# Up projections of the middle block as seven block products, with new weight sums and a spilled convolution

## The chip, the cores and the metric

One of the cores of a Trainium2 chip runs the program. The metric is the device time of one execution in microseconds; the time of a kernel is the median of several runs. TensorE (PE) multiplies, VectorE (DVE) and ScalarE (ACT) do the element-wise work, GpSimd (POOL) does little here, and SyncE (SP) issues every DMA, in the order of the program, on one queue.

## The reference

One layer of a hybrid decoder works on 2128 positions (16 meta tokens, 2048 prompt tokens, 64 sample tokens) of 1024 channels, in float32. A token-mixing block (input projection to 5 x 1024 columns, a causal convolution of width 31 with a layer norm, a pooling branch, gates, an output projection) is followed by a gated feed-forward part. The feed-forward part is what the change touches most:

```python
h2 = rmsnorm(x, norm2_g)
up = h2 @ w_up                                  # 1024 -> 2 x 2816
up, new_ffn = causal_dwconv(up, prev_ffn, ffn_dw)   # width 3
v, g = up[..., :D_FF], up[..., D_FF:]
x = x + (jax.nn.gelu(g) * v) @ w_down           # 2816 -> 1024
```

## The kernel before

**Tiling.** Channels lie on the 128 partitions (8 chunks, index c), positions on the free axis. The positions are cut into three blocks b of 708, 708 and 712; a matmul takes one half of a block (354 or 356 columns, 356 or 358 with the two columns of history that the width-3 convolution needs). The sample tokens are the last 64 columns of block 2.

**Precision.** Each operand is split into a high part of type fp32r (copied by ACT) and the remainder (subtracted by DVE). A product of two such operands is three matmuls: low x high, high x low, high x high. All of PE's work on weights has line L212.

**Units and tasks.** The program is a list of units, each one weight tile with its matmuls and the work on its results. For block b the order is: pooling and gate projections (PG), convolution projections (C), output projection (WO), for b = 1 then the gate and value projections of block 2 (G), and the feed-forward part (FF). FF works on value/gate couples f = 0 to 21, in groups; the down projection (DN) of a group is placed behind the first couple of the next group, and the last one at the end (`up_end` marks its start). Norms, convolutions (`conv_norm`, `conv_pair`), weight sums and the like are tasks, generators that `drip` steps in order of their creation while DVE's planned time (class `Pace`) is behind PE's. `force` finishes a task that a unit needs. A task can yield until `room(k)` holds: at most 52 tiles of one size, "s" in the profile, share one pool, and three are kept in reserve.

**Weights.** A weight tile ("wb") holds both parts, 2 x 1024 columns, 1 MB. There are four such buffers (`W_BUFS`, L51), taken in turn. A weight is loaded as "raw" and split when it is used for the first time, and the split tile is stored to HBM ("keep"). Later uses load it from there. `w_loads` (L275) issues the loads in the order of use, at most LEAD = 4 units ahead of the unit last named to `w_start` (L311), and one unit fewer for weights that are known in HBM. A load into a buffer has to wait for the last matmul that reads the tile that was there.

**Pairs.** In block 2 (`MIXED`), the couples f = 3 to 21 are computed by `pair` (L964): the 8 input chunks are seen as 2 halves and the two halves of the columns as 2 halves, so that value and gate of one couple are a 2 x 2 block product, computed with 7 block products of 12 matmuls instead of 8. The operands are sums: `mixed_rows` makes those of the activations, the task `mixed_weights` those of the weights, seven parts of 512 columns for each f, split, and stored in HBM in the order of use (m1 to m3 of two parts, m4 of one). A pair uses its four PSUM banks x, a, bb, d in this order:

```python
prod(x, 0, 0, b11, True)
prod(a, 0, h, mx[1], True)
prod(bb, 1, 0, mx[3], True)
prod(d, 1, h, mx[2], True)
prod(x, 2, 0, b21, False)
prod(bb, 2, h, mx[4], False)
prod(a, 3, 0, b22, False)
```

The second argument is the number of the weight tile (0 for m1 to 3 for m4). After product 4, DVE forms a sum that is shared, and the value and the gate come out of five such sums, of 358 columns each. Block 2 works in groups of 6, 6, 5, 5 couples (`MIX_GROUPS`), blocks 0 and 1 in groups of 6, 5, 5, 6, where a couple is two plain units of 48 matmuls.

**Order around the change.** `mixed_weights` starts with PG of block 1, is the last in the list of tasks, and is barred from WO of block 1 to shortly after the start of G. The convolutions of block 2 can start in G and end in FF of block 1. In `MIXED` blocks the residual x1 is kept in HBM between groups (`spill`, `fetch`).

## Time and profile before

| what | us |
|---|---|
| median of 3 runs | 3002.84 |
| lowest, highest run | 2999.94, 3004.23 |
| the profiled execution, its own time | 3004.2 |
| its span, first to last instruction | 3002.1 |
| busy PE | 2938.3 |
| busy DVE | 2042.8 |
| busy ACT | 821.2 |

The span is the stretch that the profile covers; the own time of that execution is 2.1 us longer. A row of the profile names the line, the engine, the operation and the tiles ("out<-in"), then the count, the busy time and the mean duration of one in ns, and at the end how long the engine was idle before and what released it. Matmuls are pipelined: the mean duration of one is longer than the distance from one to the next. Lines L180, L184 and L195 are helpers through which nearly all of DVE's and ACT's work goes, so that tiles tell more than lines.

Where the stages of blocks 1 and 2 begin (first L212 matmul, us from the start of the span): PG of block 1 at 1155, C at 1309, WO at 1434, G at 1499, FF at 1627; PG of block 2 at 2150, C at 2294, WO at 2418, FF at 2483.

### The profile page before, as it was taken

What the parts mean: (1) busy time and instruction counts of PE and PEld (TensorE: products, weight loads), DVE (VectorE), ACT (ScalarE), POOL (GpSimd) and SP (SyncE); (2) the same over time, 40 slices, a digit from 0 to 9 for tenths busy, and PEclk for the clock granted to TensorE, in tenths of its full rate; (3) what the DMA queues carried; (4) which work ended last, traced back from release to release, by engine and by line L of the source; (5) the groups of instructions that cost most, each with busy time, mean ns of one, the idle gap of its engine ahead of it and who ended that gap; (6) DMA issues with size and microseconds to landing.
All of it is one profiled execution on the core that took longest, in us unless ns stands there. A gap on an engine that the chain in (4) does not pass through costs nothing.

```text
span 3002.1 us, 44205 instructions
## 1 busy us (share of the span) xinstructions
PE 2938.3 (98%) x17928; PEld 2924.6 (97%) x17928; DVE 2042.8 (68%) x3006; ACT 821.2 (27%) x1238; POOL 108.8 (4%) x201
## 2 busy tenths in 40 slices
PE   7999999999999998999999999999999999999998
PEld 7999999999999998999999999999999999999997
DVE  7998998679996456653489999655652137544645
ACT  4201334233223232432221212223241113221312
POOL 0111100020000000000010000000000000000000
PEclk9999999999999999999999999999999999999999
DMA  7424554955655557888743444799743376777686
GB/s 283 160 71 161 196 207 162 335 212 173 229 189 197 204 191 286 274 321 277 277 154 120 163 136 146 266 320 328 266 170 138 139 267 215 255 268 263 236 302 242
DMA packets 187755, 660.41 MB, mean 220 GB/s; under 512 B 30880, under 2 KB 39200, under 8 KB 145696
## 3 DMA queue, kind: packets, MB, share of 16 engines
q1 hardware_dynamic: 187552, 657.59, 62.2%
q8 instruction: 141, 2.31, 0.3%
q14 instruction: 62, 0.51, 0.0%
HBM read 433.35 MB, written 224.17 MB: 219 GB/s over the span
## 4 chain that ended last, share of the span: by engine, by line
PE 81%; DVE 12%; ACT 2%; DMA 2%; issue 2%; SPq 0%; DVEq 0%; ACTq 0%
PE ps L212 81%; DVE s L184 8%; DVE s L180 2%; DVE wb L180 2%; ACT s L195 2%; DMA wb<-keep 1%; DMA s<-in_x 0%; ACT wb L195 0%; DMA out_ffn_s<-sf 0%; DMA raw<-in_w_in 0%; SPq L204 0%; DVE s L189 0%; DMA raw<-in_w_dn 0%; SPq L208 0%; DVE rs L184 0%
## 5 line engine op out<-in xcount | busy, mean ns | idle before, releaser
L212 PE MATMUL ps<-s,wb 128*128 128x356 f32 (+2 forms) x17628 | 2904.4, 326 | 32.3 <-DMA wb<-keep 11.7
L212 PEld LDWEIGHTS ps<-s,wb 128*128 128x128 f32 x17628 | 2886.3, 189 | 43.2 <-DVE s L180 19.4
L184 DVE SCALAR_TENSOR_TENSOR s<-s,half,s 128x708 f32<-128x708 f32 (+1 forms) x720 | 622.5, 928 | 0.0
L195 ACT ACTIVATE s<-s 128x708 fp32r<-128x708 f32 (+8 forms) x447 | 316.2, 715 | 829.9 <-DVE s L184 465.8
L180 DVE TENSOR_TENSOR s<-s,s 128x708 f32<-128x708 f32 (+10 forms) x526 | 402.4, 779 | 102.5 <-ACT s L195 92.7
L180 DVE TENSOR_TENSOR s<-s,ps 128x708 f32<-128x708 f32 (+4 forms) x225 | 159.7, 719 | 289.9 <-PE ps L212 233.5
L195 ACT ACTIVATE s<-ps 128x358 f32<-128x358 f32 (+4 forms) x197 | 117.5, 603 | 696.4 <-PE ps L212 679.8
L184 DVE SCALAR_TENSOR_TENSOR s<-ps,cst,s 128x708 f32<-128x708 f32 (+1 forms) x188 | 179.0, 953 | 91.6 <-ACT s L195 88.0
L184 DVE SCALAR_TENSOR_TENSOR s<-s,cst,s 128x712 f32<-128x712 f32 (+3 forms) x188 | 156.5, 845 | 88.2 <-ACT s L195 81.0
L180 DVE TENSOR_TENSOR wb<-raw,wb 128x1024 fp32r<-128x1024 f32 (+3 forms) x136 | 152.9, 1126 | 41.0 <-ACT wb L195 40.6
L195 ACT ACTIVATE wb<-raw 128x1024 fp32r<-128x1024 f32 (+3 forms) x136 | 132.2, 977 | 157.4 <-PE ps L212 92.3
L195 ACT ACTIVATE s<-ps,cst 128x708 f32<-128x708 f32 (+1 forms) x94 | 79.4, 847 | 272.9 <-PE ps L212 266.5
L184 DVE SCALAR_TENSOR_TENSOR s<-s,ps 128x708 f32<-128x708 f32 (+5 forms) x65 | 43.8, 695 | 144.1 <-PE ps L212 124.8
L184 DVE SCALAR_TENSOR_TENSOR s<-s,s 128x708 f32<-128x708 f32 (+2 forms) x96 | 85.5, 891 | 73.4 <-ACT s L195 71.6
L180 DVE TENSOR_TENSOR s<-raw,s 128x512 fp32r<-128x512 f32 x114 | 74.5, 687 | 60.8 <-ACT s L195 52.5
L195 ACT ACTIVATE s<-raw 128x512 fp32r<-128x512 f32 x114 | 68.2, 626 | 86.9 <-DMA raw<-in_w_up 68.7
L180 DVE TENSOR_TENSOR s<-s 128x722 f32<-128x722 f32 (+6 forms) x64 | 55.3, 863 | 28.2 <-ACT s L195 20.5
L200 POOL COPY s<-phist 128x15 f32<-128x15 f32 x24 | 16.5, 687 | 1080.4 <-PE ps L212 1023.8
L184 DVE SCALAR_TENSOR_TENSOR sc<-sa,cst,sc 128x64 f32<-128x64 f32 x232 | 46.9, 280 | 0.3
L195 ACT ACTIVATE s<-s,half 128x708 f32<-128x708 f32 (+1 forms) x48 | 46.5, 975 | 0.8
L195 ACT ACTIVATE s<-s,cst 128x712 f32<-128x712 f32 x38 | 33.7, 886 | 40.4 <-DVE s L180 38.4
L200 POOL CAST s<-hhist 128x2 fp32r<-128x2 f32 x48 | 17.5, 396 | 607.8 <-PE ps L212 389.8
(51 smaller groups left out, 369.5 us busy)
## 6 DMA issues: line engine op xcount, KB each, us to landing
wb<-keep SPq DMA_DIRECT2D x227, 1024.0 KB, 5.0
keep<-wb SPq DMA_DIRECT2D x100, 1024.0 KB, 6.3
keep<-s SPq DMA_DIRECT2D x266, 256.0 KB, 5.7
raw<-in_w_up SPq DMA_DIRECT2D x82, 512.0 KB, 5.7
wb<-keep SPq DMA_DIRECT2D x40, 640.0 KB, 5.2
wb<-keep SPq DMA_DIRECT2D x32, 768.0 KB, 5.2
raw<-in_w_in SPq DMA_DIRECT2D x40, 512.0 KB, 5.2
s<-in_x SPq DMA_DIRECT2D x40, 354.0 KB, 7.6
```

The costliest lines, as they stand in the source:

```text
L180: nc.vector.tensor_tensor(out=out, in0=a, in1=b, op=op)
L184: nc.vector.scalar_tensor_tensor(out=out, in0=a, scalar=s, in1=b, op0=op0, op1=op1)
L195: nc.scalar.activation(out, a, func, **kw)
L200: nc.gpsimd.tensor_copy(out, a)
L212: nc.tensor.matmul(out, lhsT=lhsT, rhs=rhs, start=start, stop=stop, skip_group_check=again)
```

## The change

Block 1 gets the pairs too, with groups of its own (5, 5, 4, 4, 4); couples 0 to 2 stay plain in both blocks. The two halves of a value and gate weight that are used unsummed are no longer stored again: a pair takes them from the split weights that block 0 stored ("up" with f, and the second half of "up" with 22 + f, called "half"). `mixed_weights`, now one task for each f, makes only the four sums, in one HBM tile of 2048 columns, of which "s13" is the first half and "s24" the second. So the seven products are computed in the same order, with other weight tiles, and the loads of the next pair are issued at other places:

```diff
-        w = [W((f"m{i}", f), None, h if i == 4 else 2 * h) for i in range(1, 5)]
+        w = [W(("up", f), A["w_up"][f]), W(("s13", f), None, 2 * h), W(("s24", f), None, 2 * h), W(("half", FC + f), None, h)]
...
             prod(x, 0, 0, b11, True)
...
-            prod(a, 0, h, mx[1], True)
-            w_start(w[1])
+            prod(a, 1, 0, mx[1], True)
...
-            prod(bb, 1, 0, mx[3], True)
+            prod(bb, 1, h, mx[3], True)
...
-            prod(d, 1, h, mx[2], True)
-            w_start(w[2])
+            prod(d, 2, 0, mx[2], True)
...
-            prod(x, 2, 0, b21, False)
+            prod(x, 0, h, b21, False)
+            w_start(w[2], 0)
...
-            prod(bb, 2, h, mx[4], False)
-            w_start(w[3])
+            prod(bb, 3, 0, mx[4], False)
...
-            prod(a, 3, 0, b22, False)
-            w_start(w[3] + 1)
+            prod(a, 2, h, b22, False)
+            w_start(w[3] + 1, 0)
```

The second argument of `w_start` is new; with 0, known weights may be loaded four units ahead, as others are.

```diff
-            if q.known and wstate["load"] >= wstate["first"] + LEAD - 1:
+            if q.known and wstate["load"] >= wstate["first"] + LEAD - wstate["late"]:
```

The weight sums, without the three unsummed parts:

```diff
-            yield from part(a11, "m1", 0, 2 * h)
-            yield from part(a12, "m3", 0, 2 * h)
-            yield from part(a22, "m3", h, 2 * h)
...
-            yield from part(s3, "m2", 0, 2 * h)
+        yield from part(s3, h)
...
-            yield from part(a21, "m1", h, 2 * h)
-            yield from part(a11, "m2", h, 2 * h)
-            yield from part(a12, "m4", 0, h)
+        yield from part(a21, 0)
+        yield from part(a11, 2 * h)
+        yield from part(a12, 3 * h)
+        kept["sums", f] = dst
```

These tasks stand ahead of the convolutions in the list now. Each pair needs the sums of its own f instead of all of them. The activations of block 1 get a norm of their own (`norm2_mixed`, which also sends the residual to HBM), and `mixed_rows` forms their sums from the split halves (`summed`).

The convolutions of block 2 ("last block") no longer stay in "s" tiles. Their inputs go to HBM when G has made them, are loaded again two chunks at a time, and the results go to HBM until the layer norm, which waits for the start of block 1's last down projection:

```diff
+            if b == SPILLED:
+                yield at(a)
+                R["ad", c] = dpool.tile([P, HC + n], F32, tag=f"ad_{c}", name=f"ad_{c}")
+                store(R["ad", c], a)
...
-        yield from room(2)
+        yield from room(4 if b == SPILLED else 2)
+        if b == SPILLED:
+            for cc in (c, c + 1):
+                a = R["a", b, cc][0] = S(HC + n)
+                load(a, R["ad", cc])
...
+        while b == SPILLED and now["i"] < mark["up_end", b - 1]:
+            yield "cond", lambda: now["i"] >= mark["up_end", b - 1]
...
+                    load(R["cv", b, cc], R["cvd", cc])
```

More of the change, by code (lines that the diff above doesn't have):

```diff
@@ L249, in trunk @@
     wsplits = {}
-    wstate = {"load": 0, "split": 0, "done": 0, "raws": 0, "first": 0}
+    wstate = {"load": 0, "split": 0, "done": 0, "raws": 0, "first": 0, "late": 1}
     def known(key):
+        if key[0] in ("s13", "s24", "half"):
+            t = kept.get((("up" if key[0] == "half" else "sums"), key[1]))
+            return None if t is None else t[:, :, :D] if key[0] == "s13" else t[:, :, -D:] if key[0] == "s24" else t[:, :, D // 2 :]
         if key[0] != "dn":
@@ L613, in conv_norm @@
                 tt(acc, acc, cv, ALU.add)
+            del cv
+            if b == SPILLED and c:
+                yield at(acc)
+                for cc in (0, 1) if c == 1 else (c,):
+                    R["cvd", cc] = dpool.tile([P, W], F32, tag=f"cvd_{cc}", name=f"cvd_{cc}")
+                    store(R["cvd", cc], R.pop(("cv", b, cc)))
+        while b == SPILLED and now["i"] < mark["up_end", b - 1]:
+            yield "cond", lambda: now["i"] >= mark["up_end", b - 1]
         yield at(acc)
@@ L622, in src @@
         def src(c):
+            for cc in range(c, min(c + AHEAD, KC)):
+                if ("cv", b, cc) not in R:
+                    yield from room(1)
+                    R["cv", b, cc] = S(W)
+                    load(R["cv", b, cc], R["cvd", cc])
             if c == 0:
@@ L865, in mixed_rows, with row_sums @@
-        del R["xt", b]
-    def mixed_weights():
+            rows = R["xt", b] if ("xt", b) in R else [summed(b, c) if c % (KC // 2) == k else None for c in range(KC)]
+            yield from row_sums(b, rows[k], rows[k + KC // 2])
+            del rows
+        R.pop(("xt", b), None)
+    def row_sums(b, x0, x1):
+        n, ops = hw(b) + 2, R["mx", b]
+        b11, b12 = halves(x0, b)
+        b21, b22 = halves(x1, b)
+        ta, tb = S(2 * n), S(2 * n)
+        t1, t2, t3, t4 = ta[:, :n], ta[:, n:], tb[:, :n], tb[:, n:]
+        tt(t1, b12, b11, ALU.subtract)
+        tt(t2, b22, t1, ALU.subtract)
+        tt(t3, b22, b12, ALU.subtract)
+        tt(t4, b21, t2, ALU.subtract)
+        del x0, x1, b11, b12, b21, b22
+        yield at(ta)
+        for t, (i, j) in ((ta, (1, 2)), (tb, (3, 4))):
+            hi, lo = S(2 * n, F32R), S(2 * n, F32R)
+            act(hi, t, AF.Copy)
+            yield at(hi)
+            tt(lo, t, hi.bitcast(F32), ALU.subtract)
+            ops[i].append((hi[:, :n], lo[:, :n], hi, lo))
+            ops[j].append((hi[:, n:], lo[:, n:]))
+            yield
@@ new lines, in mixed_weights, with part @@
+        yield from room(MIX_ROOM)
+        v, g = (pace.alloc("raw", RAW_BUFS, wpool.tile([P, 2 * h], F32, tag="raw", name=nm("raw"), bufs=RAW_BUFS)) for _ in range(2))
+        load(v, A["w_up"][f])
+        load(g, A["w_up"][FC + f])
+        a11, a12, a21, a22 = v[:, :h], v[:, h:], g[:, :h], g[:, h:]
+        yield at(g)
+        dst = dpool.tile([P, 2, 4 * h], F32, tag=f"sums_{f}", name=f"sums_{f}")
+        def part(t, c):
+            calm = lambda: pace.free["dma"] < pace.free["pe"]
+            yield "room", calm
+            yield from room(MIX_ROOM)
+            hi, lo = S(h, F32R), S(h, F32R)
+            act(hi, t, AF.Copy)
+            yield at(hi)
+            tt(lo, t, hi.bitcast(F32), ALU.subtract)
+            yield at(lo)
+            store(dst[:, 0, c : c + h], hi.bitcast(F32))
+            store(dst[:, 1, c : c + h], lo.bitcast(F32))
@@ L1317, in FF @@
         mark["FF", b] = len(units)
-        ws = [w_up(0), w_up(FC), w_up(1)]
+        plain = PLAIN.get(b, FC)
+        ws = [w_up(0), w_up(FC), w_up(1)] if plain else []
         holds = [[] if len(parts) > 1 else None for _ in ws]
-        for ts_ in parts:
+        for ts_ in parts if plain else ():
             i = len(units)
@@ L1326, in FF @@
         f0, pend = 0, None
-        for gs in MIX_GROUPS if b in MIXED else F_GROUPS:
+        for gs in MIX_GROUPS.get(b, F_GROUPS):
             for f in range(f0, f0 + gs):
-                if b in MIXED and f >= PLAIN:
+                if f >= PLAIN.get(b, FC):
                     pair(b, f)
@@ L1369, in trunk @@
         for ts_ in parts.get(b, (BOTH,)):
-            add_task(("h2", b, ts_), norm2(b, ts_))
+            add_task(("h2", b, ts_), norm2_mixed(b) if b in MIXED and ts_ == BOTH else norm2(b, ts_))
         if b in MIXED:
-            add_task(("mx", b), mixed_rows(b), after=[("h2", b, parts[b][-1]), ("mw",)])
+            add_task(("mx", b), mixed_rows(b), after=[("h2", b, parts.get(b, (BOTH,))[-1])])
         for ts_ in SPLIT if b == NBLK - 1 else (BOTH,):
@@ L1378, in trunk @@
             if b + 1 == SBLK:
+                for f in range(min(PLAIN.values()), FC):
+                    add_task(("mw", f), mixed_weights(f), mark["PG", 1], [("mw", f - 1)] if f > min(PLAIN.values()) else ())
                 for c in range(KC):
@@ L1470, in trunk @@
         for i, q in reversed(list(enumerate(wq))):
[L1471 removed]
+            parts_ = [("dn", q.key[1], f) for f in range(*q.key[2:])] if q.key[0] == "dn" else [("up" if q.key[0] == "half" else q.key[0], *q.key[1:])]
             q.again = all(k in last for k in parts_)
```

120 lines of the change are left out of this document (62 added, 58 removed).

## The prediction

> **What bounds the kernel now.** I read the page first, then the stages, then single pairs of units in the timeline.
>
> ```profile
> PE 2938.3 (98%) x17928; PEld 2924.6 (97%) x17928; DVE 2042.8 (68%) x3006; ACT 821.2 (27%) x1238; POOL 108.8 (4%) x201
> ...
> PE 81%; DVE 12%; ACT 2%; DMA 2%; issue 2%; SPq 0%; DVEq 0%; ACTq 0%
> ...
> L212 PE MATMUL ps<-s,wb 128*128 128x356 f32 (+2 forms) x17628 | 2904.4, 326 | 32.3 <-DMA wb<-keep 11.7
> ```
>
> PE is busy in 98% of the span and waits little, so the time is the number of matmuls times their spacing, plus PE's waits. Columns of the next view (stages, by the order of the L212 matmuls): PE, PEld, DVE, ACT, POOL busy, clock, DMA share, GB/s. The rows are block 2's gate and value projections with block 1's second norm; block 1's feed-forward part; block 2's pooling part.
>
> ```profile
> 1512.00:1637.00 125.00, 125.00 (x774) 125.00 (x773) 120.14 (x355) 20.46 (x33) 9.37 (x33) 1.00 0.43 154
> 1637.00:2162.00 525.00, 522.95 (x3217) 522.25 (x3217) 408.67 (x530) 135.36 (x192) 0.20 (x1) 1.00 0.65 224
> 2162.00:2303.00 141.00, 140.59 (x866) 140.13 (x865) 65.60 (x96) 46.60 (x74) 7.25 (x15) 1.00 0.50 175
> ```
>
> Block 1's feed-forward part, where the change lands, is bound by PE; DVE has 116 us free in it and 75 us in the stage behind it. Now PE's own timeline, the first row from block 1, the others from block 2's pairs:
>
> ```profile
> 1639.78 222.44 PE L212 MATMUL ps<-s,wb 128*128 128x356 f32 x1360
> ...
> 2589.70 72.99 PE L212 MATMUL ps<-s,wb 128*128 128x358 f32 x446
> 2663.23 14.11 PE L212 MATMUL ps<-s,wb 128*128 128x358 f32 x84 [0.54 <-DVE s L180]
> 2677.87 14.11 PE L212 MATMUL ps<-s,wb 128*128 128x358 f32 x84 [0.54 <-DVE s L180]
> ```
>
> The spacing is 222.44/1360 = 0.1636 us in block 1 and 72.99/446 = 0.1637 in block 2, so a product of a pair (12 matmuls) takes 1.96 us. A pair of block 2 is 84 matmuls, 13.75 us, but pairs follow each other by 2677.87 - 2663.23 = 14.64: each loses 0.89 us at one place, its sixth product, behind DVE's sum of product four.
>
> **Part 1, what is removed.** Nineteen of block 1's 22 value/gate couples shrink from 96 matmuls to 84: 228 fewer, 228 x 0.1636 = **-37.3 us**, all on the path.
>
> **Part 2, the weight buffers.** This step decides. A pair has four weights in a ring of four buffers, loaded in order on SP's queue. Before, each is used by neighbouring products: m1 by 1 and 2, m2 by 3 and 4, m3 by 5 and 6, m4 by 7. SP's timeline in the same pairs:
>
> ```profile
> 2665.51 0.32 SPq L204 DMA_DIRECT2D wb<-keep  x1
> ...
> 2667.52 0.38 SPq L204 DMA_DIRECT2D wb<-keep  x1
> ...
> 2671.43 0.32 SPq L204 DMA_DIRECT2D wb<-keep  x1
> ...
> 2675.39 5.08 SPq L204 DMA_DIRECT2D wb<-keep  x2
> ```
>
> Product 6 starts at 2663.23; 6 ends at 2665.20, 7 at 2667.16, and the next pair's 2 and 4 at 2671.09 and 2675.02. The loads go out 0.31 to 0.37 us after just these ends: **a load is issued when the last product on its buffer is over** (0.33 us below). The next pair's m1 leaves five products, 9.8 us, before its use.
>
> After the change, weight 1 ("up") serves products 1 and 5, weight 2 ("s13") 2 and 3, weight 3 ("s24") 4 and 7, weight 4 ("half") 6. The next pair's "up" can only go out after product 5 and is wanted after 6 and 7, that is 3.93 us later. "s13" stands behind it on SP and is wanted 5.89 us after product 5. Two loads of that size, issued back to back into an idle queue (SP's timeline, then the DMA issues of two short windows; the last column is the time to landing):
>
> ```profile
> 2509.69 0.82 SPq L204 DMA_DIRECT2D wb<-keep  x2
> ```
>
> ```profile
> wb<-keep SPq DMA_DIRECT2D x1, 1024.0 KB, 4.7
> ```
>
> ```profile
> wb<-keep SPq DMA_DIRECT2D x1, 1024.0 KB, 6.9
> ```
>
> The second is issued 0.49 us after the first and lands 7.4 us after the first's issue. From landing to matmul, in the chain of waits:
>
> ```profile
> 2170.02 6.26 DMA wb<-keep
> 2176.28 0.14 issue
> 2176.41 3.66 PE ps L212 x21
> ```
>
> So with product 5's end as zero, product 1 can start at 0.33 + 4.7 + 0.13 = 5.16 instead of 3.93, and product 2 at 0.33 + 7.4 + 0.13 = 7.86 instead of 5.89. "s24" goes out at 3.93 + 0.33 and is wanted at 7.86 + 2 x 1.96 = 11.78, 7.5 us later: in time. **Each step from pair to pair waits 7.86 - 5.89 = 1.97 us.** In block 2 the old 0.89 us lies inside this wait (it falls on product 6, after zero), so the net there is 1.08.
>
> The groups (5, 5, 4, 4, 4) with plain couples 0 to 2, and a down projection behind the first pair of each later group, give 14 such steps in block 1: 14 x 1.97 = **+27.6**. Block 2 keeps (6, 6, 5, 5), but runs the same new pair: 15 steps, 15 x 1.08 = **+16.2**. The other pairs follow plain units or a down projection, whose weights come earlier; five of them are in block 1, where each may lose block 2's 0.89: 0 to 4.4, I take **+2**, since block 1 has no sample columns in that DVE chain. Nine times a pair is followed by a down projection whose first weight (512 to 768 KB) replaces "up". Alone it lands about 3.4 to 4.05 us after issue (an estimate: 4.7 less the missing KB at the 2.7 us that the second megabyte took above); with 0.46 around it, that is 0 to 0.6 past 3.93: **+2**, bounds 0 to 6.
>
> The Trainium skill, DMA: Bandwidth & Descriptors, section "Anatomy of one DMA", fits 2.0 us plus bytes over 436 GB/s: an estimate of 4.4 us for one such load and 2.4 for the next one's bytes. The trace's 4.7 and 2.7 are worse on both, so the sum goes by the trace; by that page the wait would be 1.4 and the whole sum about nothing.
>
> **Part 3, DVE.** Rows by shape:
>
> ```profile
> L184 DVE SCALAR_TENSOR_TENSOR s<-s,half,s 128x648 f32<-128x648 f32 x240 | 197.6, 887 | 0.0
> ...
> L180 DVE TENSOR_TENSOR s<-s,ps 128x708 f32<-128x708 f32 x88 | 76.8, 888 | 93.6 <-PE ps L212 93.5
> L180 DVE TENSOR_TENSOR s<-raw,s 128x512 fp32r<-128x512 f32 x114 | 74.5, 687 | 60.8 <-ACT s L195 52.5 <-PE ps L212 6.1 <-DMA keep<-s 1.3
> ...
> L180 DVE TENSOR_TENSOR s<-s,ps 128x358 f32<-128x358 f32 x57 | 29.8, 523 | 37.1 <-ACT s L195 21.7 <-PE ps L212 15.3
> ...
> L180 DVE TENSOR_TENSOR s<-s,s 128x358 f32<-128x358 f32 x50 | 25.7, 528 | 0.8
> ```
>
> Block 1 adds five half-width sums per pair (19 x 5 x 0.525 = 50 us), the row sums (4 x 8 x 0.525 + 8 x 0.9 = 24) and eight adds for a fifth group (7). The weight sums fall from 11 DVE operations of 0.69 for each f to 8, and start as tasks ahead of the convolutions. How far they got before the window in which they are barred (DVE and ACT operations on their raw tile; ten of DVE's for one f):
>
> ```profile
> 1150.00:1200.00 50.00, 7.82 (x12) 4.69 (x8) 0.90 0.83 304
> ...
> 1350.00:1400.00 50.00, 13.21 (x20) 6.18 (x11) 1.00 0.99 340
> 1400.00:1450.00 50.00, 2.06 (x3) 1.88 (x3) 1.00 0.74 266
> ```
>
> About two f per 50 us at a DMA share up to 0.99. With 12 instead of 18 transfers of 256 KB worth for one f the same pace makes 13 or 14 of 19 there, the rest in the next projections, ahead of the convolutions. Before, ten f (76 us of DVE) fell behind 1446; after, about five (28). The three stages above held 594 us of DVE work in 791; they get 50 + 24 + 7 - 48 = 33 more. This is hidden under PE: **0**, with 164 us of cover. The 0.8 us of one convolution tap ahead of a pair's sum also lies inside the new 1.97 us.
>
> **Part 4, DMA.** Block 1's pairs load 3.5 MB in some 15.7 us, about 230 GB/s; the stages of the page ran at up to 340. On SP's queue come: eight stores of "a" (347 KB) during block 2's projections; eight loads of them and eight stores of results (365 KB) in the pairs; eight loads back while the last down projection and the pooling part run; residual spills per group, beside down projections, as block 2 has them now. Sixteen transfers in the pairs at 2.7 us a megabyte are about 1 us each when they stand ahead of a wanted weight: 0 to 16, I take **+4** for one in four. Block 2's small state transfers (40 KB, two in and two out per pair) meet the new loads too: 0 to 15, **+3**.
>
> **Sum:** -37.3 + 27.6 + 16.2 + 2 + 2 + 3 + 4 = +17.5. The profiled execution (span 3002.1, its own time 3004.2) becomes 3021.7; it stood 1.4 above the median 3002.84, so I forecast **3020 us** (own range 3009 to 3035).
>
> **Rivals.** (a) *The second load comes sooner*, that is, "s13" lands a plain 4.7 us after its own issue at 0.82 and only "up" is waited for: 1.23 per step, 14 x 1.23 + 15 x 0.34 - 37.3 + 11 = -4, **2999**. For it: the queue is idle at that moment. Against: the 6.9 above, with the queue idle too. Chance 0.16. The Trainium skill's fit, cited in part 2, leads to about the same place. (b) *Loads in time, faster*: if "up" went out two products earlier, only block 2's DVE wait would remain in block 1: -37.3 + 19 x 0.89 + 2 = -18, **2984**. It decides at 3.93 us from release to use; against it, no megabyte in the rows above lands in under 4.7. Chance 0.14. (c) *The convolutions starve*: each channel pair needs four free buffers of 52, while h2, row sums and f hold some 40. A channel pair is 60 x 0.823 = 49 us of DVE (197.6/240). One unfinished pair fits into the 75 us free in the pooling part beside the layer norm; from the second on, block 2's convolution projection waits 49 us: **3069**. Chance 0.10. (d) *No matmul goes*, or the waits cancel elsewhere: **3003**, 0.04.
>
> **How the numbers follow.** Forecast 0.56. A measurement of this kernel can tell about 0.2%, 6 us, from no change. Faster: (b) and a fifth of (a), 0.17. Same: the rest of (a), (d), and the forecast's low end, 0.21. Slower: 0.62. The range 2990 to 3045 takes in (a), the bounds of parts 2 and 4 and half of (c); it leaves out (b).
>
> **What the changed profile would show.** L212's matmuls: 17,400. In both blocks' pairs, PE idle of about 1.2 us before product 1 and 0.7 before product 2, both released by DMA wb<-keep, and SP issuing two loads together 0.33 us after product 5; pair to pair 15.7 to 15.9 us. The 0.54 us behind DVE goes where a pair follows a pair. keep<-s falls from 266 stores to 152. I am wrong if "up" is issued well before product 5 ends, if PE idles behind DVE or at the convolution projection, or if block 2's pairs stay at 14.64.

## The result and the profile after

The changed kernel takes 3042.11 us (median of 4 runs, 3034.23 to 3042.36), the kernel before 3003.53 in the same session (4 runs). The ratio is 1.0123, with an interval of 1.0104 to 1.0142. The span of the profiled execution went from 3002.1 to 3040.6 us: **+38.5**, where the forecast had +17.5. Slower was right and the time lies in the range, but the loss is more than twice what was forecast, and it came by other waits; that the range holds it is luck.

The page of the changed kernel, the lines that were shown of before (line numbers have moved by one: L213 is the matmul, L181 and L185 are DVE's, L196 is ACT's):

```profile
PE 2925.5 (96%) x17700; PEld 2900.5 (95%) x17700; DVE 2082.2 (68%) x3116; ACT 831.5 (27%) x1281; POOL 100.0 (3%) x169
...
PE 29%; DVE 7%; DMA 5%; ACT 1%; issue 1%; SPq 0%; DVEq 0%; ACTq 0%
...
L213 PE MATMUL ps<-s,wb 128*128 128x354 f32 (+2 forms) x17400 | 2891.0, 328 | 83.3 <-DMA wb<-keep 25.2
```

The matmuls that were to go are gone: 17,628 - 17,400 = 228. But PE's idle time ahead of them grew from 32.3 us to 83.3. (The chain's shares add up to 43% here; the chain was followed back over less than half of the span, so I don't read it.) Where the time came from shows by stage. I counted the L213 matmuls in their order, which gives each stage's start and length:

| stage | before, us | after, us | difference | forecast |
|---|---|---|---|---|
| FF of block 1 | 523.2 | 549.5 | +26.3 | about -2 |
| PG of block 2 | 143.8 | 151.3 | +7.5 | 0 |
| FF of block 2 | 505.8 | 512.7 | +6.9 | about +20 |
| all else | | | -2.2 | 0 |

So the two feed-forward parts missed in opposite directions. The windows of FF of block 1 and of PG of block 2 (columns as in the prediction):

```profile
1624.00:2174.00 550.00, 504.33 (x2949) 495.46 (x2949) 453.77 (x618) 138.74 (x222) 1.47 (x2) 0.97 0.80 278
...
2174.00:2325.00 151.00, 148.04 (x912) 147.24 (x912) 83.70 (x135) 49.13 (x77) 9.97 (x16) 0.99 0.46 165
```

PE was busy for 522.95 of 525 us there before and is idle for 46 of 550 now; the DMA share went from 0.65 to 0.80, and the granted clock from 1.00 to 0.97. PE's waits in that stage (us in total, times, longest):

```profile
PE ps L213 <- DMA wb<-keep: 13.8, 5, 4.3
PE ps L213 <- DVE s L181: 11.1, 7, 3.2
PE ps L213 <- issue: 10.5, 4, 3.2
PE ps L213 <- DMA wb<-sums: 5.5, 6, 1.6
PE ps L213 <- ACT s L196: 4.6, 3, 2.8
```

There is no single wait: DMA and DVE share it. (The "issue" ones lie at the same place as DVE's, ahead of product 6.) The 19 pairs of block 1 take 316.1 us together; 1596 matmuls at the spacing of 0.1638 us are 261.4. So 54.7 us are lost in them; the plain couples ahead of them lose another 7.3.

**The loads do not go out as forecast.** PE's and SP's timelines over one step between pairs of block 2:

```profile
2688.93 8.18 PE L213 MATMUL ps<-s,wb 128*128 128x358 f32 x48 [0.82 <-DMA wb<-sums]
2697.64 6.16 PE L213 MATMUL ps<-s,wb 128*128 128x358 f32 x36 [0.54 <-DVE s L181]
2705.37 8.17 PE L213 MATMUL ps<-s,wb 128*128 128x358 f32 x48 [1.56 <-DMA wb<-sums]
```

```profile
2689.38 4.37 SPq L209 DMA_DIRECT2D out_ffn_s<-sf  x2
2693.86 0.37 SPq L205 DMA_DIRECT2D wb<-keep  x1
2697.14 0.53 SPq L205 DMA_DIRECT2D wb<-sums  x1
...
2699.90 0.53 SPq L205 DMA_DIRECT2D wb<-sums  x1
2701.87 0.52 SPq L205 DMA_DIRECT2D wb<-keep  x1
```

Product 2 starts at 2688.93, so 3 ends near 2692.9 and 5 at 2696.8. "up" goes out at 2693.86, behind two small stores on SP, about 3 us before product 5 ends. It took the buffer of "s13", free after product 3. "s13" goes out 0.34 us after product 5, into the buffer of "up"; "s24" after product 6 and "half" after 7. A new tile takes the buffer that comes free first; the four are not used in turn. "up" is never late; "s13" alone is tight, with the 36 matmuls of products 6, 7 and 1 between its issue and its use. (So the words "taken in turn" in the description of the kernel are wrong.) The wait ahead of product 2 came (0.82 and 1.56 us here; 0.7 was forecast), the one ahead of product 1 didn't, and the 0.54 behind DVE stayed.

**In block 1, DVE comes late to its sum.** DVE's timeline up to the shared sum, and PE's product 6 behind it:

```profile
1797.34 1.69 DVE L185 SCALAR_TENSOR_TENSOR s<-s,half,s 128x648 f32<-128x648 f32 x2
1798.95 0.89 DVE L181 TENSOR_TENSOR s<-s,s 128x708 fp32r<-128x708 f32 x1
1799.76 0.68 DVE L181 TENSOR_TENSOR s<-raw,s 128x512 fp32r<-128x512 f32 x1
1800.36 0.89 DVE L185 SCALAR_TENSOR_TENSOR s<-s,half,s 128x648 f32<-128x648 f32 x1
1801.16 0.52 DVE L181 TENSOR_TENSOR s<-s,ps 128x356 f32<-128x356 f32 x1
```

```profile
1801.73 15.39 PE L213 MATMUL ps<-s,wb 128*128 128x356 f32 x84 [3.25 <-DVE s L181]
```

PE stands still for 3.25 us while DVE finishes the pair before, three convolution taps and a weight sum; only then comes the shared sum of 0.52 us. Product 6 doesn't use that sum. It writes the accumulator bb, which lies in the same PSUM tile as d, which the sum reads, and the dependency is kept by tile.

**PG of block 2** grew in every run that keeps the change (148.8 to 154.1 us, run 4 with a plain block 1 too), partly because work moved into it: of the layer norm's sums and broadcasts over c, before had 12 and 12 matmuls there and the others in FF, after has all 24 and 24. PE's groups of that stage, after and then before:

```profile
L213 PE MATMUL ps<-ones,s 128*128 128x1 f32 x24 | 3.1, 258 | 0.8 <-DVE s L181 0.8
L213 PE MATMUL ps<-cst,rs 128*128 128x128 f32 x24 | 3.0, 275 | 0.0
```

```profile
L212 PE MATMUL ps<-cst,rs 128*128 128x128 f32 x12 | 1.5, 275 | 0.0
L212 PE MATMUL ps<-ones,s 128*128 128x1 f32 x12 | 1.4, 243 | 0.0
```

That is 3.2 us of PE's work, gone from FF; the small matmuls also break up the stream at each change of kind.

### The profile page after: what moved, and what is told of

It reads as the page before. It is cut to its first block, busy times and chain, and to the rows that moved or that the text cites. A ratio compares the mean times of both kernels' runs of the same rounds, so it can differ in the third digit from the quotient of the medians.

```text
span 3040.6 us, 43827 instructions
## 1 busy us (share of the span) xinstructions
PE 2925.5 (96%) x17700; PEld 2900.5 (95%) x17700; DVE 2082.2 (68%) x3116; ACT 831.5 (27%) x1281; POOL 100.0 (3%) x169
## 5 line engine op out<-in xcount | busy, mean ns | idle before, releaser
L213 PE MATMUL ps<-s,wb 128*128 128x354 f32 (+2 forms) x17400 | 2891.0, 328 | 83.3 <-DMA wb<-keep 25.2
L213 PEld LDWEIGHTS ps<-s,wb 128*128 128x128 f32 x17400 | 2862.0, 190 | 105.2 <-DVE s L181 36.9
L185 DVE SCALAR_TENSOR_TENSOR s<-s,half,s 128x708 f32<-128x708 f32 (+1 forms) x720 | 625.2, 928 | 0.0
L196 ACT ACTIVATE s<-s 128x708 f32<-128x708 f32 (+9 forms) x463 | 323.2, 707 | 844.7 <-DVE s L185 436.6
L181 DVE TENSOR_TENSOR s<-s,s 128x708 fp32r<-128x708 f32 (+10 forms) x592 | 435.0, 750 | 93.6 <-ACT s L196 83.3
L181 DVE TENSOR_TENSOR s<-s,ps 128x708 f32<-128x708 f32 (+4 forms) x290 | 196.0, 684 | 299.2 <-PE ps L213 227.0
L196 ACT ACTIVATE s<-ps 128x356 f32<-128x356 f32 (+5 forms) x273 | 151.9, 564 | 781.8 <-PE ps L213 771.0
L185 DVE SCALAR_TENSOR_TENSOR s<-s,cst,s 128x708 f32<-128x708 f32 (+3 forms) x264 | 229.3, 877 | 102.6 <-ACT s L196 93.9
L181 DVE TENSOR_TENSOR wb<-raw,wb 128x1024 fp32r<-128x1024 f32 (+3 forms) x136 | 152.8, 1126 | 42.4 <-ACT wb L196 42.0
L196 ACT ACTIVATE wb<-raw 128x1024 fp32r<-128x1024 f32 (+3 forms) x136 | 132.2, 977 | 159.7 <-PE ps L213 87.1
L185 DVE SCALAR_TENSOR_TENSOR s<-ps,cst,s 128x708 f32<-128x708 f32 (+1 forms) x112 | 106.7, 954 | 66.0 <-ACT s L196 63.6
L185 DVE SCALAR_TENSOR_TENSOR s<-s,ps 128x708 f32<-128x708 f32 (+5 forms) x65 | 43.9, 695 | 144.4 <-PE ps L213 144.2
L185 DVE SCALAR_TENSOR_TENSOR s<-s,s 128x708 f32<-128x708 f32 (+2 forms) x96 | 85.4, 891 | 78.0 <-ACT s L196 76.2
L196 ACT ACTIVATE s<-s,cst 128x708 f32<-128x708 f32 (+1 forms) x76 | 67.2, 884 | 124.7 <-DVE s L181 116.9
L196 ACT ACTIVATE s<-ps,cst 128x708 f32<-128x708 f32 (+1 forms) x56 | 47.4, 848 | 148.3 <-PE ps L213 148.3
L181 DVE TENSOR_TENSOR s<-s 128x722 f32<-128x722 f32 (+8 forms) x84 | 64.3, 782 | 21.0 <-ACT s L196 14.8
L185 DVE SCALAR_TENSOR_TENSOR sc<-sa,cst,sc 128x64 f32<-128x64 f32 x232 | 47.5, 280 | 1.0 <-ACT sc L196 0.7
L196 ACT ACTIVATE s<-s,half 128x708 f32<-128x708 f32 (+1 forms) x48 | 46.5, 975 | 0.8
L181 DVE TENSOR_TENSOR s<-raw,raw 128x512 f32<-128x512 f32 x19 | 13.1, 689 | 47.3 <-DMA raw<-in_w_up 47.3
L181 DVE TENSOR_TENSOR s<-raw,s 128x512 fp32r<-128x512 f32 x57 | 37.5, 685 | 6.9 <-PE ps L213 6.1
L196 ACT ACTIVATE s<-raw 128x512 fp32r<-128x512 f32 x57 | 35.3, 628 | 18.3 <-DMA xd<-s 15.6
```

The costliest lines, as they stand in the source:

```text
L181: nc.vector.tensor_tensor(out=out, in0=a, in1=b, op=op)
L185: nc.vector.scalar_tensor_tensor(out=out, in0=a, scalar=s, in1=b, op0=op0, op1=op1)
L196: nc.scalar.activation(out, a, func, **kw)
L213: nc.tensor.matmul(out, lhsT=lhsT, rhs=rhs, start=start, stop=stop, skip_group_check=again)
```

## The experiments

Theory 1: DVE's queue is overfull in block 1's pairs, because the kernel's own planner (`Pace`) makes the forecast's mistake: it hands out the buffers in turn. Theory 2: weight loads are late there, by the crowded HBM and by the late issue of "s13". Where a run's own time is compared with another session, before's medians of 3000.86 to 3003.53 say how far sessions differ.

**1. The planner takes the buffer that is free earliest, whole program.**

```diff
-            old = self.log.get(ring[-bufs], {})
-            end = max((max(v) for v in old.values()), default=(0.0, ""))
+            ends = [max((max(v) for v in self.log.get(name, {}).values()), default=(0.0, "")) for name in ring]
+            k = ends.index(min(ends)) if tag == "wb" else 0
+            end = ends[k]
+            del ring[k]
```

> The changed kernel with one edit in the planner: a new weight tile is planned into that one of the four buffers that comes free first, instead of taking them in turn. The instructions are the same, only their order on the queues differs. Theory 1 (planned pace): the plan believed that a pair takes 16.3 to 17.0 us and packed that much work onto DVE, so that PE waits at product 6 for DVE. Planned right, a pair gets at most 14 us of DVE work: the waits at product 6 in block 1 fall from 32 us in sum to under 12, block 1's feed-forward part from 549 us to about 505, the whole to 2990 to 3005. Theory 2 (weights and HBM traffic hold PE, DVE only shows it): the loads stay where they are, the time stays within 10 us of 3042.

Measured 3091.54 us, ratio 1.0302 (1.0285 to 1.0319): both expected totals failed. Block 1's pairs fell from 316.1 to 298.5 us and their stage from 549.5 to 532.3 (505 was expected), but other stages lost more, above all PG of block 0 (207.5 to 242.3). The edit took buffers that are loaded and not yet read for free ones. Run 5 mends this.

**2. Other PSUM neighbours in a pair** (x with bb, a with d):

```diff
-            x, a, bb, d = ps1[:, 0, :n], ps1[:, 1, :n], ps2[:, 0, :n], ps2[:, 1, :n]
+            x, a, bb, d = ps1[:, 0, :n], ps2[:, 0, :n], ps1[:, 1, :n], ps2[:, 1, :n]
```

> The changed kernel with the PSUM banks of a pair dealt out anew: x and bb share one tile, a and d the other, so that the shared sum (it reads d) stands in the way of product 7 instead of product 6. Theory 1: the wait moves by one product (1.96 us): in block 1 the 14 waits at product 6 (32 us) shrink by up to 1.96 each, about 22 us less with the lowered clock behind the long ones, and block 2 loses the 0.7 at nearly each pair, about 12 us; the whole 3005 to 3015. Theory 2: no wait depends on it, within 5 us of 3042.

Measured 3041.0 us, ratio 1.0129 (1.0114 to 1.0144): nothing gained. In block 2's pairs the waits for DVE went and those for "s13" nearly doubled (7.3 to 13.5 us); pairs 282.8 to 277.8. In block 1 the waits for DVE only turned into others:

```profile
PE ps L213 <- DMA wb<-sums: 16.2, 16, 2.1
PE ps L213 <- ACT s L196: 16.1, 15, 2.6
PE ps L213 <- DMA wb<-keep: 15.9, 8, 4.8
```

**3. Two of the 30 further taps of block 2's convolution** (the other taps are left out):

```diff
-        for k in range(CW - 1):
+        for k in range(2 if b == SPILLED else CW - 1):
```

> The changed kernel with only 2 of the 30 further taps of block 2's convolution on the prompt columns; the other 28 are left out, and with them 224 DVE operations of 0.82 us (184 us). The loads and stores of the spilled convolution stay. Theory 1: DVE has no filler in block 1's pairs, the waits at product 6 fall to about 0.7 each, block 1's feed-forward part goes from 549 to about 500, the whole to 2990 to 3000. Theory 2: the traffic is unchanged, so block 1's part stays over 530 and the whole over 3025.

Measured 3028.19 us, ratio 1.0086 (1.0065 to 1.0106). With 175 us of DVE work out of the stage, the waits for DVE in it are 0.6 us, and still it keeps most of its loss (534.2 us):

```profile
PE ps L213 <- DMA wb<-keep: 23.6, 8, 9.1
PE ps L213 <- DMA wb<-sums: 13.1, 10, 2.8
PE ps L213 <- DVE s L181: 0.6, 1, 0.6
```

So DVE is not the whole cause. Behind it stand the loads.

**4. Block 1 plain again, all else of the change kept.**

```diff
-PLAIN = {1: 3, 2: 3}
-MIX_GROUPS = {1: (5, 5, 4, 4, 4), 2: (6, 6, 5, 5)}
+PLAIN = {2: 3}
+MIX_GROUPS = {2: (6, 6, 5, 5)}
```

> The change without its first part: block 1 stays plain (its own pairs are left out), while block 2's pairs take their weights as changed, the weight sums are the new ones and the convolution is spilled. It prices what the change costs outside block 1's pairs. Theory 1: block 2's part stays 5 to 9 us longer than before and block 1's is as before, the whole 3005 to 3015. Theory 2: the spills and the weight sums in block 1's feed-forward part disturb plain units too, so that it takes over 535 us instead of 523, the whole over 3018.

Measured 3013.84 us, ratio 1.0039 (1.0024 to 1.0054). Block 2's new weights, the sums and the spill cost 12 us by themselves (before had 3001.63 in that session); block 1's pairs cost 26 on top (38.6 - 12.2), with 228 matmuls fewer.

**5. The planner told of the right buffer**, one whose weight has been read for the last time; and **6.** the same with the PSUM neighbours of run 2.

```diff
-            old = self.log.get(ring[-bufs], {})
-            end = max((max(v) for v in old.values()), default=(0.0, ""))
+            end = lambda name: max((max(v) for v in self.log.get(name, {}).values()), default=(0.0, ""))
+            name = min([x for x in ring if x in self.used] or ring[:1], key=end) if tag == "wb" else ring[-bufs]
...
+            pace.used.update(wq[w[j]].both.tensor.name for j in (0, 1))
             w_start(w[2], 0)
```

> Edit: the planner is told which weight buffer really comes free first (in a pair: after products 3, 5, 6 and 7), and counts a buffer as free only once its weight has been read for the last time; nothing else changes. It differs from the earlier edit of the plan, which also took buffers that were loaded and not yet read as free. Theory 1 (the planner believes that weights come late, so it fills VectorE to the brim of an imagined 16.3-us pair, and TensorE then waits for a queued VectorE at product 6): block 1's pairs fall from 316 us to about 298, the waits for VectorE inside them nearly vanish, other stages stay within 3 us of the changed kernel's, total about 3023 (3015 to 3030). Theory 2 (block 1's pairs wait for weight loads on a crowded HBM, whatever the plan): the pairs stay above 308 us with the waits now at the loads, total 3033 to 3045.

> Edit: the plan as in the run beside it, and the two accumulators that VectorE's shared sum and product 6 use lie in different PSUM buffers. If the 0.7-us wait at product 6 in block 2's pairs is the shared buffer, block 2's FF stage falls from 513 to about 508 and the total is 4 to 8 us below the run beside it (3010 to 3025 by theory 1); if block 1's pairs are bound by loads, block 1 gains nothing from the swap.

**7. One set of weight sums** (the first; all pairs load it, the other 18 are not made: there are 19, f = 3 to 21, not the 20 of the expectations), with the plan of the change; and **8.** with the plan of run 5.

```diff
+        if f > min(PLAIN.values()):
...
+            kept["sums", f] = kept["sums", f - 1]
+            return
```

> Edit: only the first of the 20 sets of weight sums is made, and every pair loads that one; the 1 MB of raw loads, the 2 MB of stores and the VectorE and ScalarE work of 19 sets are left out. The plan is as in the changed kernel. Theory 2 (HBM traffic of the sums): the waits for weight loads in block 1's pairs go, landing of the sums falls from 7 us to 5, FF stage of block 1 from 549 to about 520 or less; the total 3005 to 3015. Theory 1: VectorE's freed time is filled with convolution taps, the waits at product 6 remain until the convolution is done (which is earlier), the FF stage 535 to 545, total 3025 to 3035.

> Edit: both of the above, one set of sums and the plan with the right buffers. If the two causes add up (VectorE's queue from the plan, loads from the traffic), block 1's pairs fall to 19 x 13.75 = 261 us and some 10 to 20 us of remaining waits, 270 to 285, and the total to 2985 to 3000. If one of them is the whole, this run equals the better of the two single ones within 4 us.

The four belong together (FF of block 1, and its pairs, us; before is 523.2 for the stage):

| | all sets: stage, pairs, median | one set: stage, pairs, median |
|---|---|---|
| plan of the change | 549.5, 316.1, 3042.1 | 537.0, 313.5, 3028.9 |
| right buffers | 536.7, 306.1, 3033.2 | 516.2, 293.8, 3005.2 |

Each alone takes some 12.5 us off the stage, both 33.3: more than their sum, as if where one limit is lifted the other holds. (Stage and pairs are those of the one profiled execution; run 8's was 5.3 us above its median.) PG of block 0 stayed at 207.5 us with the right buffers, so run 1's loss there was the wrong choice of buffer. Theory 1's own total (3023) was missed: the waits for DVE fell, and those for "s13" grew in their place (ahead of product 2, 2.5 to 13.1 us). The plan is seen in the place of the waits ahead of product 6: in the 14 steps from pair to pair they fall from 23.6 us to 1.5, in the five pairs behind plain units or a down projection they rise from 8.8 to 16.0. Run 5's waits in the stage:

```profile
PE ps L217 <- DMA wb<-sums: 14.9, 14, 3.7
PE ps L217 <- DMA wb<-keep: 13.8, 5, 4.4
PE ps L217 <- DVE s L185: 8.3, 3, 4.3
```

Run 7 stands at 1.0087 (1.0066 to 1.0107), run 8 at 1.0001 (0.9991 to 1.0012). Run 6 (3031.83 us, 1.0096, 1.0081 to 1.0111) is no better than run 5 (1.0106, 1.0090 to 1.0123), and the single set with the right plan (2985 to 3000 was expected) still loses 32 us in its pairs, 12 of it waiting for "s13" and 6 for "s24".

**9. Products 4 and 5 change places**, on top of run 5, so that "up" is free a product earlier and "s13" goes out 48 matmuls ahead of its use instead of 36. Two more edits belong to this run: x shares its PSUM tile with d now, and a with bb; and the sums of the next pair are finished (`force`) before the loads that "up" sets free. **10.** The same with one set of sums. **11.** Run 9, with the weight sums allowed between WO of block 1 and G too. **12.** The kernel before, with run 2's neighbours.

```diff
-            x, a, bb, d = ps1[:, 0, :n], ps1[:, 1, :n], ps2[:, 0, :n], ps2[:, 1, :n]
+            x, a, bb, d = ps1[:, 0, :n], ps2[:, 0, :n], ps2[:, 1, :n], ps1[:, 1, :n]
...
-            prod(d, 2, 0, mx[2], True)
-            box["n"] = 4
-            posts.append(Task("post", sums()))
-            yield
...
             prod(x, 0, h, b21, False)
+            if ("mw", f + 1) in tasks:
+                force(("mw", f + 1))
...
             w_start(w[2], 0)
+            yield
+            prod(d, 2, 0, mx[2], True)
             box["n"] = 5
+            posts.append(Task("post", sums()))
             yield
```

```diff
-        return posts + ws + [t for t in rest if not (quiet and t.name[0] in ("cv", "sc") or norm and t.name[0] == "mw")]
+        return posts + ws + [t for t in rest if not (quiet and t.name[0] in ("cv", "sc"))]
```

> Edit: the plan with the right buffers, and products 4 and 5 of a pair change places (the second product with the up weight comes fourth), so the up weight's buffer is free one product earlier: the next s13 is issued 48 matmuls ahead of its product 2 instead of 36, 7.85 us instead of 5.89, and the next s24 60 instead of 48. Product 1 and the fourth accumulator share a PSUM buffer, the other two the other one. Theory 2a (what is left of block 1's pairs are loads that land 6.5 to 8 us after an issue 5.9 us ahead of use, and in block 2 as well): the waits for sums go in both blocks, block 2's pairs fall from 282 us to 268 to 272, block 1's from 306 to 285 to 292, total 3000 to 3010. Theory 2b (the HBM's throughput is the limit, 3.5 MB a pair and the rest beside it, so that an earlier issue only lands later): both change by less than 5 us, total 3025 to 3035.

> Edit: as the run before it, and only one set of weight sums made (19 sets of raw loads, stores and VectorE work left out). By 2a block 1's pairs come close to 19 x 13.75 = 261 us (262 to 272, against 293.8 without the new order) and the total to 2965 to 2980, so the whole loss is the three things together: plan, weight sums inside the pairs, s13 issued late. By 2b the pairs stay above 288 and the total above 2998.

> Edit: as the first run of this call, and the weight sums may also run in the stages from block 1's output projection to block 2's gate and value projections, where the changed kernel holds them back; so fewer of them fall into block 1's pairs. If their place is what costs (up to the 20 us between one set and all sets), the total falls by 5 to 15 us below the first run of this call; if VectorE and the HBM are merely as full there, the convolution is pushed into the pairs in their stead and the total stays within 4 us.

> Edit: the kernel before, with only the accumulators of the pairs (block 2) placed so that VectorE's shared sum and product 6 use different PSUM buffers. If the 0.7-us wait before product 6 in each of the 19 pairs is that shared buffer, the pairs fall from 275 us to 263 to 267 and the total to 2990 to 2996; if the waits only move to the next reader of a buffer, 3000 to 3004.

| run | median, us | ratio to before (interval) | pairs of block 1 | pairs of block 2 |
|---|---|---|---|---|
| 9, new order | 2999.48 | 0.9993 (0.9983 to 1.0002) | 292.6 | 263.8 |
| 10, new order, one set | 2964.57 | 0.9872 (0.9853 to 0.9892) | 272.1 | 262.1 |
| 11, sums early | 2992.90 | 0.9975 (0.9964 to 0.9986) | 274.3 | 263.3 |
| 12, before, neighbours | 2990.31 | 0.9960 (0.9946 to 0.9975) | none | 263.0 |

Run 9 takes 34 us off run 5. In block 2 nothing is left: PE runs through a whole group of pairs (its timeline),

```profile
2654.80 105.42 PE L217 MATMUL ps<-s,wb 128*128 128x358 f32 x641
```

so there the product order and the shared PSUM tile, mended together, were the whole loss, and the HBM carries the 3.5 MB of each pair. In block 1 the pairs still lose 31 us, 23 of them in the four pairs that follow a down projection (22.2, 18.4, 17.7 and 19.6 us instead of 13.75). The first of these, on PE, on SP, and in the DMA of that stretch:

```profile
1768.66 16.77 PE L217 MATMUL ps<-s,wb 128*128 128x356 f32 x84 [5.47 <-DMA wb<-sums]
```

```profile
1746.90 1.01 SPq L213 DMA_DIRECT2D sums<-s  x2
...
1754.78 1.40 SPq L213 DMA_DIRECT2D sums<-s  x2
1756.39 1.25 SPq L209 DMA_DIRECT2D raw<-in_w_up  x2
1758.54 0.33 SPq L209 DMA_DIRECT2D s<-xd  x1
1759.09 0.52 SPq L209 DMA_DIRECT2D wb<-sums  x1
```

```profile
DMA packets 3143, 9.14 MB, mean 365 GB/s; under 512 B 310, under 2 KB 310, under 8 KB 3013
...
wb<-sums SPq DMA_DIRECT2D x2, 1024.0 KB, 9.8
```

"s13" is issued at 1759.09 behind stores of sums, spills and raw weights, while the DMA engines move 365 GB/s, and lands after 9.4 us instead of 4.7. But it also goes out late: the buffer that it takes is free when the sixth of the down projection's eight units ends, at 1751.4, 11.6 us before product 2 wants it. Issued then, even a load of 9.4 us would have been in time. Run 10, without 18 sets, has 10.7 us lost in the pairs. Run 11 takes 18 us from block 1's pairs against run 9, of which 7 come back in G (127.5 to 134.3).

**13. VectorE's work of 18 sets without their transfers** (constants instead of the raw weights, nothing stored), on run 9; **14. and 15. the stores of the sums issued by ScalarE**, on run 11 and on run 9; **16. and 17. the raw loads of the sums issued by GpSimd**, on run 9 and on run 11.

```diff
-        load(v, A["w_up"][f])
-        load(g, A["w_up"][FC + f])
+        if f > min(PLAIN.values()):
+            nc.gpsimd.memset(v, 1.0)
+            nc.gpsimd.memset(g, 1.0)
...
+            if f == min(PLAIN.values()):
...
+        kept["sums", f] = dst if f == min(PLAIN.values()) else kept["sums", f - 1]
```

```diff
-            store(dst[:, 0, c : c + h], hi.bitcast(F32))
-            store(dst[:, 1, c : c + h], lo.bitcast(F32))
+            store(dst[:, 0, c : c + h], hi.bitcast(F32), nc.scalar)
+            store(dst[:, 1, c : c + h], lo.bitcast(F32), nc.scalar)
```

```diff
-        load(v, A["w_up"][f])
-        load(g, A["w_up"][FC + f])
+        load(v, A["w_up"][f], nc.gpsimd)
+        load(g, A["w_up"][FC + f], nc.gpsimd)
```

> Edit: as the run with the right plan and the exchanged products, and for 19 of the 20 sets of weight sums the two raw loads and the eight stores are left out while VectorE and ScalarE do all the set's work on constants (every pair loads the first set). All sets: block 1's pairs 292.6 us, total 2999.5; one set: 272.1 us, 2964.6. If the sets cost by their HBM traffic, this run is near the one set: pairs 270 to 278, total 2964 to 2975. If they cost by VectorE's time (the convolution pushed on into the pairs), it is near all sets: pairs 286 to 294, total 2990 to 3000.

> Edit: as the run that lets the weight sums run early (2992.9 us), and the eight stores of each set are issued by ScalarE instead of SyncE, so that they don't stand ahead of weight loads on SyncE. If the order on SyncE's queue is what makes the weights late beside the sums (the 4 to 5-us waits for a kept weight ahead of block 1's first products, in G2 and in the first projection), block 1's plain products and G2 lose some 5 us each and block 1's pairs a few, total 2975 to 2985. If HBM throughput is it, the loads land as late as before: 2989 to 2996; if ScalarE is held up by stores that wait for VectorE, 2996 to 3010.

> Edit: the run with the right plan and the exchanged products (2999.48 us, block 1's pairs 292.6, with all weight sums inside the pairs), and the eight stores of each set are issued by ScalarE instead of SyncE. Same bytes, another queue. If the sums cost by standing ahead of weight loads on SyncE's queue, the pairs fall to 272 to 280 and the total to 2972 to 2985. If they cost by the bytes that move while the weights are wanted, the pairs stay within 5 us of 292.6 and the total within 6 us of 2999.5.

> Edit: the run with the right plan and the exchanged products (2999.48 us, block 1's pairs 292.6, its plain couples 55.0), and the two raw loads of each set of weight sums are issued by GpSimd instead of SyncE; the stores stay on SyncE. A raw load waits for its buffer, which VectorE frees; on SyncE, whatever stands behind it waits too (in the runs so far SyncE issues nothing for about 4 us ahead of such a pair of loads, just before the 4 to 5.5-us waits for sums). If that head of the queue is what costs, the pairs fall to 272 to 282, the plain couples to 47 to 50, the total to 2972 to 2987. If the bytes cost, pairs and total stay within 5 and 6 us of that run.

> Edit: the same raw loads by GpSimd in the run that lets the sums run early (2992.9 us). By the head of the queue, the waits for a kept weight in G (5 us) and ahead of block 1's first products (5 us) go and the pairs lose a few: 2975 to 2983, faster than any version so far. By the bytes: 2989 to 2996.

| run | median, us | ratio to before (interval) | pairs of block 1 |
|---|---|---|---|
| 13, DVE's work only | 2965.06 | 0.9873 (0.9854 to 0.9893) | 271.3 |
| 14, sums early, stores by ACT | 2995.39 | 0.9978 (0.9968 to 0.9988) | 273.1 |
| 15, stores by ACT | 3002.36 | 1.0003 (0.9993 to 1.0012) | 293.0 |
| 16, raw loads by POOL | 2997.97 | 0.9990 (0.9981 to 1.0000) | 286.5 |
| 17, sums early, raw loads by POOL | 2989.07 | 0.9965 (0.9952 to 0.9978) | 276.6 |

Run 13 equals run 10 with all of VectorE's work of the sums done, so the total of VectorE's work is not what the sums cost. But with no transfers to wait for, that work all ran before 1400, ahead of block 1's pairs; run 13 doesn't say what the same operations cost inside them. Three of the 19 sets fall there in run 9.

Run 15 equals run 9 and run 14 equals run 11, and in run 16 the pairs lost 6 us less than in run 9, just over the 5 that stood for "bytes". So taking either the stores or the raw loads off SyncE's queue gains little. That doesn't clear the queue: what is left on it still holds "s13". The long wait on PE in run 16, then SP's timeline in run 15, where the raw loads hold the queue ("xd" is the spilled residual), and in run 13, with neither:

```profile
1766.15 16.13 PE L217 MATMUL ps<-s,wb 128*128 128x356 f32 x84 [3.92 <-DMA wb<-sums]
```

```profile
1751.88 0.32 SPq L213 DMA_DIRECT2D xd<-s  x1
1756.32 1.60 SPq L209 DMA_DIRECT2D raw<-in_w_up  x2
1759.04 0.33 SPq L209 DMA_DIRECT2D s<-xd  x1
1759.78 0.53 SPq L209 DMA_DIRECT2D wb<-sums  x1
```

```profile
1736.78 0.72 SPq L209 DMA_DIRECT2D wb<-sums  x1
```

In run 13 the "s13" of this pair (f = 6) goes out at once when its buffer is free, lands after 7.7 us and isn't waited for. In runs 9, 15 and 16 it goes out 7.7, 7.4 and 5.7 us after that. The same holds for f = 11: 5.1 us late and a load of 8.6 in run 9, when 11.5 were there. In these two pairs, with 8.0 us of waits ahead of product 2 in run 9, the late issue makes the wait: even the slowest of these loads, 9.9 us in run 16 at 358 GB/s, would have been in time if it had gone out at once. In run 11 the "s13" of f = 6 takes 9.8 us to land and PE doesn't wait, since it goes out 0.8 us after its buffer is free. No run takes both the stores and the raw loads to other queues, none makes the transfers without VectorE's work, and none takes the spill's bytes away: how the 21 us between runs 9 and 13 divide between the queue, the bytes and the place of VectorE's work stays open.

The same 200 us inside block 1's pairs in the kernel before, the changed one, run 9 and run 13:

```profile
1680.00:1880.00 200.00, 200.00 (x1224) 199.56 (x1223) 195.04 (x240) 41.81 (x58) 0.00 (x0) 1.00 0.41 139
```

```profile
1680.00:1880.00 200.00, 176.60 (x1020) 172.62 (x1019) 175.51 (x234) 49.42 (x83) 0.00 (x0) 0.96 0.80 272
```

```profile
1680.00:1880.00 200.00, 193.44 (x1161) 191.14 (x1160) 165.54 (x220) 48.90 (x82) 0.00 (x0) 0.98 0.86 287
```

```profile
1680.00:1880.00 200.00, 198.52 (x1211) 196.77 (x1211) 182.31 (x237) 49.15 (x82) 0.00 (x0) 1.00 0.85 292
```

PE, its first busy column, goes 200.00, 176.60, 193.44, 198.52. Run 13 has more DVE work in the stretch than the changed kernel (182 against 176 us), and about the same DMA rate, yet PE hardly waits: with the plan and the order mended, neither a busy DVE nor the mean DMA rate is a limit by itself in this stretch. (Over the whole stage run 13 has less DVE work than run 9, 406 us against 447.) It is the stretches like the one above that hurt.

**The fastest versions** that compute all are run 12 (0.9960), run 17 (0.9965) and run 11 (0.9975), all faster than both kernels; their intervals overlap. Run 12 is the kernel before with one line changed, so pairs in block 1, mended as far as these runs went, have not yet paid for themselves.

## Why the prediction was wrong, point by point

**Part 1, right.** 17,400 matmuls, 228 fewer, 37.3 us off PE.

**Part 2, the step that failed.** "The next pair's "up" can only go out after product 5 and is wanted after 6 and 7": it rests on buffers taken in turn. SP's timeline shows "up" issued near the end of product 3. So only "s13" is left to wait for, with 5.56 us from its issue (0.33 after product 5) to its use. The term of +27.6 us in block 1 measured 2.5 (the waits ahead of products 1 and 2 in its pairs), and 13.1 in run 5, where DVE no longer holds PE back ahead of them. In block 2, where the sums are all made, the new cost was +6.9 us, not +16.2 and +3 for the state transfers. The order of the products was still what decides, as the forecast said: run 9, whose new order comes with new PSUM neighbours, took 18 us from block 2's pairs and 13.5 from block 1's (against run 5).

The trace of before held the hint: the stated rule, "a load is issued when the last product on its buffer is over", was read from weights that come free in the order of loading, where both ways of choosing look alike.

**Part 3, wrong in block 1.** "This is hidden under PE: 0, with 164 us of cover" counted DVE's work against the length of the stages. DVE's sum of work indeed fitted, but its order didn't: the planner, which charges its loads to buffers in turn, plans the pair's period by the very wait that the forecast believed in. By the kernel's formulas (size over 340 GB/s plus 2.0 us a load, 0.13 between engines), "up" lands 5.34 us after product 5 and "s13" at 8.43; with four products more, a pair lasts 16.3 us instead of 13.75. `drip` fills that length with taps, and PE stands 0.7 to 3.8 us ahead of product 6 in each of the first 14 pairs, f = 3 to 16 (32 us together, where the forecast had 0 to 4.4); the last five, when the taps are used up (the last ends at 2031.7), don't wait there. The right buffers took 10 us from block 1's pairs (run 5), and 19.7 where 18 sets of sums were out of the way too (313.5 to 293.8, runs 7 and 8). "I am wrong [...] if PE idles behind DVE", the forecast said; it does.

**Part 4, mis-sized.** +7 us were put down for transfers, of the spill and of the small states. The weight sums' transfers were left out of block 1's pairs: the forecast had the sums done in block 2's projections, ahead of FF. Of the 19 sets two fall into the plain couples of FF and three into the pairs. The windows of DVE's and ACT's operations on raw tiles in the changed kernel (DVE busy and count, ACT busy and count, clock, DMA share, GB/s) show the last of them deep in the pairs, until about 1950:

```profile
1860.00:1950.00 90.00, 2.06 (x3) 1.89 (x3) 0.98 0.87 293
1950.00:2050.00 100.00, 0.00 (x0) 0.00 (x0) 0.97 0.75 260
```

With plan and order mended, leaving these transfers out is worth 292.6 - 271.3 = 21 us in the pairs, and 8 more in the plain couples ahead of them (55.0 to 46.9), by their bytes and by their places on SyncE's queue; with nothing mended, leaving out the sums is worth 12.5 in the stage.

**The stage behind.** PG of block 2 was put at 0; it costs 7.5 us, 3.2 of them matmuls of the layer norm that moved there from FF, out of FF's account. The rest was not taken apart.

**Signs.** Right: 17,400 matmuls, 152 stores of sums. Wrong: no idle before product 1, no two loads together after product 5, the wait behind DVE not gone, block 1's pairs 16.6 us apart in the mean (the 15.7 to 15.9 forecast for a step come close, by other waits).

**Rivals.** (a) needs a wait for "up", which didn't come; the fit that the prediction sets beside it (the Trainium skill, DMA: Bandwidth & Descriptors, section "Anatomy of one DMA") is one for DMAs issued by GpSimd, and these loads go out on SyncE. (b), "up" out two products earlier, was right about the load; its time was missed because DVE's lateness and the traffic took the place of the wait. Its 19 x 0.89 us behind DVE shows in run 12, which takes 12.3 us off the pairs by another PSUM neighbour. (c), starving of buffers, did not show: the last convolution tap ended at 2031.7, before FF's end.

## What to carry to other kernels

Read which buffer a load gets from a trace in which the tiles come free out of order, or treat "in turn" as a guess: here the forecast and the kernel's own planner shared it, and the planner turned a wait that didn't exist into one that did, by filling VectorE. Before a dense stage is given fewer matmuls, ask which transfers it used to hide: block 1's plain products hid the weight sums' transfers, and pairs that load 3.5 MB each could not. When a load is late, look whether it landed slowly or was issued late behind others on its queue, and take the whole queue away before clearing it. When single repairs each give less than expected, try them together before dropping either.

## What the runs showed of the hardware

PE's clock drops after shorter idling than I had expected. A row of PE's timeline in the changed kernel:

```profile
2009.09 15.46 PE L213 MATMUL ps<-s,wb 128*128 128x356 f32 x84 [2.12 <-DMA wb<-keep]
```

At 0.1636 us, 84 matmuls and the last one's tail (0.17) are 13.9 us; this stretch takes 1.6 us more, after idling for 2.12 us. The granted clock is 0.60 from 2009 to 2013 and 1.00 from 2017 to 2024. Other stretches after 2 to 3 us ran at full speed, such as the 60 that took 10.03 us after 2.70 (a granted clock of 1.00 from 1819.8 to 1823.8). By the distances from matmul to matmul, seven runs of 11 to 20 slow ones, about 0.30 us apart, cost 12.1 of the 54.7 us in block 1's pairs, and the granted clock is 0.97 in that stage. The Trainium skill, TensorE: Matmul & The Clock Gate, section "HAM oscillation — how this bites in real kernels", warns of idle gaps over about 3.4 us; this trace shows that 2.1 us can be enough.

A load of 1 MB that took 4.7 us from issue to landing on an idle queue takes 7.0 in the median of "s13" and "s24" in the changed kernel, and 9.4 and 10.2 for the two in run 9's 25 us, where the DMA engines move 365 GB/s.
